# Three transformer mixers on one core: the slab of x, the raw weights and the temporary tiles move to the other end of the on-chip memory

## The chip, the cores and the metric

The kernel runs on one core of a Trainium2 chip. A core has five engines that run side by side: TensorE (PE, matmuls; its weight loads are listed as PEld), VectorE (DVE), ScalarE (ACT), GpSimd (POOL) and SyncE (SP, which issues most DMAs). They work on SBUF, an on-chip memory of 128 partitions; a tile takes the same bytes in each partition, and its address is the byte at which it begins there. The metric is the device time of one execution in microseconds (us), as the median of three runs; less is better.

## What is computed

Two programs in a row, on 512 tokens of 1024 features, in float32:

```
x = x + merged(windowed attention, gated convolution) @ w_out     # first mixer
x = x + moe(rmsnorm(x))           # 32 experts, 2 for each token
for layer in range(2):
    h = h + mixer(rmsnorm(h))     # two kinds of full attention; then neighbourhood attention
    h = h + relu(rmsnorm(h) @ w_up)**2 @ w_down     # w_up 1024 x 4096, w_down 4096 x 1024
out = rmsnorm(h)
```

## The kernel before

Features lie on partitions and the 512 tokens along the free dimension. Nearly all products are of 128 x 128 blocks of a weight with 128 x 512 blocks of activations. For precision each operand is kept as two float32r tiles, a rounded part and the rest: `wh` and `wl` for weights, `xh` and `xl` (or `uh` and `ul`, `mh` and `ml`, and so on) for activations. One block is then three matmuls into the same PSUM bank: `wh` with `xh`, `wh` with `xl`, `wl` with `xh` (`mm3`, lines 222 to 226). The 128 x 128 weight block is loaded into the array (PEld), and the 512 columns of the activation block are streamed through it.

Weights come as a stream that all phases draw from. `_dma` loads a job (1 MB for most) into one of three `raw` tiles; `_split` lets ScalarE round 512 columns of it into one of four `wh` tiles (line 122), and `_lows` lets VectorE put the rest into `wl` (line 131), a few blocks ahead of TensorE. `raw`, `wh` and `wl` are rings: a slot is used again as its last reader is done.

The phases are the first mixer (to about 340 us), the experts (to 650), the first full attention (to 910), the first feed-forward layer (to 1273), neighbourhood attention (to 1535) and the second feed-forward layer. In a feed-forward layer `ffn` alternates between `up`, in which 4 banks of 8 blocks each are formed from `xh` and `xl`, and `down`, in which 8 banks of 4 blocks each are formed from `uh` and `ul`; that is 96 matmuls in either. The experts use float32 weights straight from the buffers that the DMAs fill (`raw`, `ew`, `esH`, `esL`, `ey`, and the tiles `t`), 2 MB for each half of a pair's gate and up, and `comb` (line 1879) adds their results `y` through one-hot matrices `C`.

Space is given out by pools. A pool on the left side grows upwards from the pools opened before it, one on the right side downwards from the top. `const`, `slab`, `wp` and `tmp` stay open from start to end. The phase pools are opened and closed on top of them. So the sizes of the pools below set the address of everything above. In `slab` lie the two activation slabs H and L (`xh`, `xl`) and one more slab, tag X, which holds `x`, and at other times `xin`, `mg`, `pt` or `V`; in `wp` lie `raw`, `wh` and `wl`; in `tmp` lie twelve small tiles `few` of 160 bytes, `ss`, seven tiles `t`, three tiles `rcol` of 32 bytes, and `rstd`.

The order of the instructions is that in which the program is written (`manual_schedule`); nothing reorders them. The lines that the change touches are those that open pools (44 to 47) and those that allocate `raw` (53) and the X slab (858, 877, 1021, 1129, 1340, 1440).

Of the kernel before, what the change touches and what calls it, by code (L numbers as in the profile page):

```python
# [16 lines left out]
T = 512  # L17
# [9 lines left out]
class Row:  # L27
    """Tiles of 512 columns as one."""
# [9 lines left out]
class Core:  # L38
    """Pools, engines and the stream of weights that every phase draws from."""

    def __init__(self, ctx, tc, aps):
# [5 lines left out]
        self.tmp = ctx.enter_context(tc.tile_pool(name="tmp", bufs=1))  # L47
# [5 lines left out]
        raw = lambda: self.wp.tile([128, 2048], F32, name="raw", tag="raw", bufs=NRAW)  # L53
# [15 lines left out]
    def add_job(self, ap, blocks, split=True, ring=0):  # L69
        """One transfer; blocks: (width, count) of the blocks in it, in order. Returns what is to be added to groups."""  # L70
        j = len(self.jobs)
        self.jobs.append((ap, ring))
        gs, off = [], 0
        for w, n in blocks:
            if not split:
                gs.append((off, w * n, w))
                off += w * n
                continue
            while n:
                k = min(n, SPL // w)  # L80
                gs.append((off, w * k, w))
                off += w * k
                n -= k
        gs = [(j, o, n, w, split, i == len(gs) - 1) for i, (o, n, w) in enumerate(gs)]
        return gs
# [41 lines left out]
    def _lows(self, upto=None):  # L127
        """The second parts that are still to be formed, up to group upto."""
# [6 lines left out]
    def blk_w(self, ahead=NSPL - 1):  # L135
        """The next block of weights in two parts; what comes after it is split ahead."""
# [22 lines left out]
    def slab_ring(self):  # L159
        """A ring of the slabs of x in two parts, while they are free."""  # L160
# [23 lines left out]
    def run(self, main):  # L184
        """main, with self.ratio steps of the side work after each of its quanta; then what is left of the side work."""
# [12 lines left out]
    def later(self, n, f):  # L198
        """f, n quanta from now."""
        self.due.append([n, f])  # L200
# [27 lines left out]
    def block(self, nk, xh, xl, acc, first=True, last=True, x0=0, ahead=NSPL - 1):  # L228
        """acc += the next nk blocks of weights times the blocks of x from x0 on."""
# [6 lines left out]
    def split(self, src, h, l, scale=None, late=0, then=None):  # L236
        """src, scaled, in two parts, the second one late quanta after the first; then() after both."""
# [20 lines left out]
    def rsqrt(self, a, shape, out=None, pool=False):  # L258
        """a ** -0.5 of a few numbers: a guess on the exponent, a step of second order and one of third order."""
# [35 lines left out]
    def token_sums(self, s, w, n, t, o):  # L295
        """Sums over the features of s [128, T] with weights w [128, n], tokens on partitions, into t[:, o:]."""
# [3 lines left out]
    def more_sums(self, s, t, first, last):  # L300
        """The sums of one tile of several into t[:, :4]."""
# [4 lines left out]
    def norm_tokens(self, s, n=D):  # L306
        """rstd of every token, tokens on partitions: [128, 4]."""
# [13 lines left out]
    def rows(self, cols, t, p0=0, p1=128):  # L321
        """cols [128, 4 or less] as a row of tokens on the partitions p0..p1 of a bank."""
# [11 lines left out]
    def norm_begin(self, g0):  # L334
        """Slabs for g * x in two parts, and a function to call as each block of x is final."""
# [10 lines left out]
    def square(self, s, x, d, dve=False):  # L346
        """s (+)= x * x; s as a list takes the last block on its own."""
# [43 lines left out]
def ffn(c, X, H, L, s, finish, halves=False):  # L391
    """X += relu(h W_up)^2 W_down, h = the norm of x; finish(d) as block d is final."""
    nc = c.nc
    c.mark("ffn")
    with c.tc.tile_pool(name="ffn", bufs=1, reuse_waits="tile") as pool:
# [44 lines left out]
        def down_halves():  # L440
            """The last chunk for one half of the tokens, then for the other."""
# [34 lines left out]
def final(c, X, out):  # L476
    """Function to call as a block of half of the tokens is final; the norm of the half follows the last one."""
# [45 lines left out]
def blocks(w, mb, kb):  # L523
    """[kb, 128, mb, 128] view of a weight."""
    return w.reshape(kb, 128, mb, 128)
# [24 lines left out]
class Heads:  # L550
    """Blocks of two heads each: gain and rope now, the scale of their norms for all of them at once.

    The scale of a token's norm commutes with gain and rope; for q it is left to the softmax.
    """
# [5 lines left out]
    def take(self, acc, g, b, write):  # L560
        """Block b from PSUM."""
# [24 lines left out]
    def scales(self, rcol):  # L586
        """The norm's scale and the main norm's in one: [128, 4, 2 n], heads of all blocks."""
# [14 lines left out]
    def scale_k(self, r, f, kst, go):  # L602
        """r * the scale of its norms, f [128, 4, 2], into kst; then go()."""
# [16 lines left out]
def v_tokens(c, acc, V, rcol):  # L620
    """Two heads of v from features to tokens on partitions, scaled."""
# [13 lines left out]
def write_q(c, r, qst, pool=False):  # L635
    """Two heads, each with its two parts one above the other; qst [128, 2, T]."""
# [7 lines left out]
def write_k(c, r, kst):  # L644
    """Two heads, each part twice; kst [128, 2 heads, 2 parts, T]."""
# [14 lines left out]
def pairs_attn(c, units, scores, scale, pv, sink=None, lag=2, ready=None):  # L660
    """Softmax attention over head pairs.

    scores(u, hh, i, nm, p) returns the scores and puts -max * scale(u, hh, i) into nm.
    """
# [122 lines left out]
class WindowPV:  # L787
    """Products with v; room holds the transposed probabilities of three heads, in turn."""
# [63 lines left out]
def window(c):  # L852
    """The first mixer, and the router's part of the experts behind it."""
# [4 lines left out]
    xin = c.slab.tile([128, NB, T], F32, name="xin", tag="X")  # L858
# [18 lines left out]
    mg = c.slab.tile([128, NB, T], F32, name="mg", tag="X")  # L877
# [42 lines left out]
    def conv(j, x, y):  # L920
        """The three taps over x * y."""
# [96 lines left out]
    def start():  # L1018
        es1.close()
        c.moe = Moe(c)  # L1020
        return c.slab.tile([128, NB, T], F32, name="x", tag="X"), {d: xres[:, d] for d in range(NB)}
# [23 lines left out]
def load_res(c, xr, res):  # L1045
    """x before a mixer."""
# [5 lines left out]
def outproj(c, mh, ml, done, start, norm, nn, early=4):  # L1052
    """x = xr + W m, block by block, and the next norm behind it.

    The first two blocks run as the parts of m come, done() of them, and early - 2 more while the last part is awaited;
    start() gives x and xr when all are there.
    """
# [48 lines left out]
class Cat:  # L1106
    """Blocks of several tiles in a row."""
# [8 lines left out]
def l0(c, nn, accs, res, norm):  # L1116
# [12 lines left out]
    ptx = c.slab.tile([128, 2, 4, T], F32, name="pt", tag="X")  # L1129
# [32 lines left out]
    def latent(n, g0, tag, keep, after):  # L1162
        """Blocks with a norm of their own: keep(m, acc, gain) takes them, after() follows the scale of the norm."""
# [170 lines left out]
def after_attn(c, es, es1, res):  # L1334
    """x, and x before the mixer, in the room of the attention."""
# [4 lines left out]
    return c.slab.tile([128, NB, T], F32, name="x", tag="X"), xr  # L1340
# [46 lines left out]
class GridPV(WindowPV):  # L1387
    """Blocks of queries half a block behind those of keys: three of them see two blocks of keys each.

    The fourth has the last 64 tokens, which see the last block, and the first 64, which see the first one.  # L1390
    Transposed probabilities lie by blocks of keys, the first one last.
    """
# [28 lines left out]
def l1(c, nn, res, norm):  # L1421
# [18 lines left out]
    V = c.slab.tile([128, 4, D], F32, name="V", tag="X")  # L1440
# [115 lines left out]
def moe_jobs(c):  # L1556
    """Three pieces for each pair of experts: two halves of gate and up, and down; each in one transfer or two."""
# [25 lines left out]
def moe_order():  # L1583
    """The pieces as they are used: the gates and ups of a pair before the down of the one before."""
# [9 lines left out]
class Moe:  # L1594
# [28 lines left out]
    def norm(self):  # L1623
        """As Core.norm_begin, for the router: logits without the norm's scale and rows of x for the gathers."""
# [28 lines left out]
    def row(self, d, xd):  # L1653
        """Block d of x, tokens as rows, for the gathers."""
# [12 lines left out]
    def first(self, name, src, mx, desc, n):  # L1667
        """One-hot of the first of the largest."""
# [10 lines left out]
    def route(self, X):  # L1679
        """1 + the position of every token among those of every expert that takes it, else 0."""  # L1680
# [50 lines left out]
    def gates(self):  # L1731
        """Gates and the norm's scale of every token for every expert, and the largest count."""
# [41 lines left out]
    def onehot(self, n, pos):  # L1774
        """Slots of the tokens for n pairs of experts."""
# [5 lines left out]
    def slots(self, n, oh, idc, idg):  # L1781
        """1 + the token of the slots of n pairs of experts, 0 for none; for the gather the token, and 0 for none."""
# [15 lines left out]
    def slots2(self, n, oh, info, gate, rs):  # L1798
        """Gate and norm's scale of the same slots."""
# [27 lines left out]
    def gu(self, xt, w, rs):  # L1827
        """silu(x Wg) * (x Wu) of the slots of a pair of experts; w(): the next half of the weights of both."""
# [24 lines left out]
    def down(self, ht, ws, gate, Y):  # L1853
        """gate * (hid Wd) in two parts."""
# [17 lines left out]
    def comb(self, X, d, slots):  # L1872
        """Block d of x += the slots of some pairs: (Y, C) of each."""
# [9 lines left out]
    def beyond(self, X):  # L1883
        """The slots past the first CAP of every expert, for inputs that fill them."""
# [43 lines left out]
    def early(self):  # L1928
        """Weights of the first experts in the room for results."""
# [4 lines left out]
def moe(c, X, nn, next_g):  # L1934
# [45 lines left out]
    def w():  # L1980
        """The next piece of the weights of both experts of a pair."""
# [96 lines left out]
def feat3(w):  # L2078
    """[L, n] -> [128, L * n / 128]"""
# [3 lines left out]
def perm(x):  # L2083
    """tokens (row, col) -> (col, row)"""
# [3 lines left out]
def mblocks(w, order, per):  # L2088
    """Blocks of 128 columns in the given order, per of them a job: [jobs, 128, per * K]."""
# [6 lines left out]
def lay_out(w, early=4):  # L2096
    """Blocks in the order of outproj, 16 to a job."""
# [120 lines left out]
```

## Time and profile before

| | |
|---|---|
| time, median of 3 runs | 1901.78 us (1900.95 to 1902.89) |
| span of the profiled execution, first to last instruction | 1899.4 us |
| TensorE busy | 1839.3 us (97%) |
| VectorE, ScalarE, GpSimd busy | 1080.8, 724.5, 341.7 us |
| DMA | 257.08 MB, mean 135 GB/s over the span |

For the profiled execution the profile gives its span; the timed runs are other executions of the same program. Times in the rows are from the start of the span. Matmuls are pipelined: one begins before the one ahead of it ends, so the time that a run of them takes is read from starts, not from the length of one. [...]

### The profile page before, as it was taken

How to read it: one execution, taken by the hardware profiler on the slowest of the kernel's cores; microseconds unless marked ns; L12 is line 12 of the kernel's file. 1: busy time of each engine (PE TensorE's matmuls, PEld its weight loads, DVE VectorE, ACT ScalarE, POOL GpSimd, SP SyncE). 2: the span in 40 equal slices, each digit the busy share in tenths (PEclk: the TensorE clock that was granted, in tenths of full speed). 3: DMA queues.
4: the chain of work that ended last, by engine and by line, in shares of the span. 5: the costliest groups of instructions: out<-in, count | busy, mean ns of one | idle time of the engine just before them, and what ended most of it. 6: DMA issues, size and time to landing. Idle time of an engine off the chain costs nothing.

```text
span 1899.4 us, 23667 instructions
## 1 busy us (share of the span) xinstructions
PE 1839.3 (97%) x8890; PEld 1370.8 (72%) x8890; DVE 1080.8 (57%) x1956; ACT 724.5 (38%) x1418; POOL 341.7 (18%) x356
## 2 busy tenths in 40 slices
PE   7999999799999999999999999999999999999998
PEld 6777787534444686667888888878777788888887
DVE  7765446535333767774655555564766565555555
ACT  4444334211111456654433333333656443333334
POOL 5310003110000251001211111120444221111111
PEclk9999999799999999999999999999999999999999
DMA  5211436599999321211323223233222222222321
GB/s 189 75 51 67 139 134 240 186 353 424 423 422 386 99 75 41 60 41 70 111 89 111 89 89 102 98 121 112 79 57 59 94 103 95 105 89 90 110 89 45
DMA packets 67334, 257.08 MB, mean 135 GB/s; under 512 B 22224, under 2 KB 28752, under 8 KB 42128
## 3 DMA queue, kind: packets, MB, share of 16 engines
q1 hardware_dynamic: 54848, 227.41, 32.5%
q0 software_dynamic: 5712, 19.66, 3.2%
q10 hardware_dynamic: 6656, 8.45, 1.2%
q8 instruction: 72, 1.18, 0.3%
q14 instruction: 46, 0.38, 0.1%
HBM read 245.28 MB, written 8.39 MB: 134 GB/s over the span
## 4 chain that ended last, share of the span: by engine, by line
PE 58%; DVE 5%; ACT 2%; issue 1%; POOLq 0%; DVEq 0%; ACTq 0%
PE psacc L224 15%; PE psacc L225 15%; PE psacc L226 15%; PE psT L693 2%; PE psO L847 2%; DVE wl L131 1%; PE psT L324 1%; PE psO L1416 1%; PE psS L224 1%; PE psS L225 1%; PE psS L226 1%; PE psT L1408 1%; PE psS L1473 1%; PE psS L1157 1%; ACT p L680 1%
## 5 line engine op out<-in xcount | busy, mean ns | idle before, releaser
L131 DVE TENSOR_TENSOR wl<-raw,wh 128x512 fp32r<-128x512 f32 x466 | 404.2, 871 | 248.6 <-ACT wh L122 244.7
L224 PE MATMUL psacc<-xh,wh 128*128 128x512 f32 x1008 | 408.9, 406 | 6.1 <-ACT wh L122 5.5
L122 ACT CAST wh<-raw 128x512 fp32r<-128x512 f32 x466 | 286.1, 617 | 334.7 <-PE psacc L225 284.0
L225 PE MATMUL psacc<-xl,wh 128*128 128x512 f32 x1008 | 396.0, 393 | 1.0 <-DVE xl L248 0.9
L226 PE MATMUL psacc<-xh,wl 128*128 128x512 f32 x1008 | 396.0, 393 | 0.1
L224 PEld LDWEIGHTS psacc<-xh,wh 128*128 128x128 f32 x1008 | 190.7, 189 | 55.9 <-issue 14.2
L226 PEld LDWEIGHTS psacc<-xh,wl 128*128 128x128 f32 x1008 | 190.6, 189 | 42.0 <-DVE wl L131 0.7
L225 PEld LDWEIGHTS psacc<-xl,wh 128*128 128x128 f32 x1008 | 191.1, 190 | 35.3 <-DVE xl L248 2.3
L224 PE MATMUL psacc<-uh,wh 128*128 128x512 f32 x480 | 190.1, 396 | 2.2 <-DVE x L436 2.2
L225 PE MATMUL psacc<-ul,wh 128*128 128x512 f32 x480 | 189.8, 396 | 0.0
L226 PE MATMUL psacc<-uh,wl 128*128 128x512 f32 x480 | 189.8, 396 | 0.0
L404 POOL TENSOR_TENSOR t<-t,rstd 128x512 f32<-128x512 f32 x64 | 83.2, 1299 | 535.1 <-ACT t L403 535.1
L436 DVE TENSOR_TENSOR x<-psacc,x 128x512 f32<-128x512 f32 x120 | 82.7, 689 | 134.4 <-PE psacc L226 134.4
L362 POOL TENSOR_TENSOR ss<-ss,t 128x512 f32<-128x512 f32 (+1 forms) x56 | 69.7, 1244 | 262.6 <-ACT t L355 242.5
L224 PEld LDWEIGHTS psacc<-uh,wh 128*128 128x128 f32 x480 | 90.2, 188 | 25.1 <-issue 3.4
L226 PEld LDWEIGHTS psacc<-uh,wl 128*128 128x128 f32 x480 | 90.2, 188 | 21.9
L225 PEld LDWEIGHTS psacc<-ul,wh 128*128 128x128 f32 x480 | 90.2, 188 | 21.5
L240 ACT CAST uh<-t 128x512 fp32r<-128x512 f32 x64 | 39.8, 621 | 131.3 <-DVE t L405 131.3
L693 PE MATMUL psT<-cst,p 128*128 128x128 f32 x448 | 77.2, 277 | 12.9 <-ACT p L680 12.7
L693 PEld LDWEIGHTS psT<-cst,p 128*128 128x128 f32 x448 | 55.2, 140 | 42.2 <-ACT p L680 22.3
L403 ACT ACTIVATE t<-psacc 128x512 f32<-128x512 f32 x64 | 38.2, 597 | 80.8 <-PE psacc L226 80.8
L701 DVE COPY pt<-psT 128x256 f32<-128x256 f32 (+1 forms) x80 | 43.2, 540 | 39.2 <-PE psT L693 38.5
(461 smaller groups left out, 2791.2 us busy)
## 6 DMA issues: line engine op xcount, KB each, us to landing
raw<-ffn SPq DMA_DIRECT2D x64, 1024.0 KB, 4.8
ew<-e_w SPq DMA_DIRECT2D x15, 2048.0 KB, 12.7
raw<-e_w SPq DMA_DIRECT2D x20, 1024.0 KB, 12.0
esH<-e_w SPq DMA_DIRECT2D x8, 2048.0 KB, 14.4
esL<-e_w SPq DMA_DIRECT2D x8, 2048.0 KB, 14.0
raw<-w_in_a SPq DMA_DIRECT2D x8, 1024.0 KB, 6.6
raw<-od_qk SPq DMA_DIRECT2D x8, 1024.0 KB, 4.8
raw<-w_gccp SPq DMA_DIRECT2D x8, 768.0 KB, 4.2
```

Of the source, the lines that this page charges most:

```text
L122: nc.scalar.copy(h[:, :n], r)
L131: self.nc.vector.tensor_sub(l, r, h)
L224: nc.tensor.matmul(acc, wh, xh, start=first, stop=False)
L225: nc.tensor.matmul(acc, wh, xl, start=False, stop=False)
L226: nc.tensor.matmul(acc, wl, xh, start=False, stop=last)
L240: nc.scalar.copy(h, src)
L362: self.nc.gpsimd.tensor_add(s, s, q)
L403: nc.scalar.activation(r, acc, AF.Relu)
L404: nc.gpsimd.tensor_mul(r2, r, st["r2"])
L436: nc.vector.tensor_add(X[:, d], acc, X[:, d])
L693: nc.tensor.transpose(t[:, o:o + 128], p[:, m * 128:m * 128 + 128], c.ident)
L701: nc.vector.tensor_copy(dst, src)
```

## The change

Two pools are new, `xs` for the slab X and `wr` for `raw`, and they and `tmp` are opened on the right side. The rest of the diff renames the pool at each allocation and takes out comments and docstrings, which moves line numbers by two behind the new pools.

```
-        self.tmp = ctx.enter_context(tc.tile_pool(name="tmp", bufs=1))
+        self.xs = ctx.enter_context(tc.tile_pool(name="xs", bufs=1, side="right"))
+        self.wr = ctx.enter_context(tc.tile_pool(name="wr", bufs=1, side="right"))
+        self.tmp = ctx.enter_context(tc.tile_pool(name="tmp", bufs=1, side="right"))
...
-        raw = lambda: self.wp.tile([128, 2048], F32, name="raw", tag="raw", bufs=NRAW)
+        raw = lambda: self.wr.tile([128, 2048], F32, name="raw", tag="raw", bufs=NRAW)
...
-    xin = c.slab.tile([128, NB, T], F32, name="xin", tag="X")
+    xin = c.xs.tile([128, NB, T], F32, name="xin", tag="X")
...
-    mg = c.slab.tile([128, NB, T], F32, name="mg", tag="X")
+    mg = c.xs.tile([128, NB, T], F32, name="mg", tag="X")
...
-        return c.slab.tile([128, NB, T], F32, name="x", tag="X"), {d: xres[:, d] for d in range(NB)}
+        return c.xs.tile([128, NB, T], F32, name="x", tag="X"), {d: xres[:, d] for d in range(NB)}
...
-    ptx = c.slab.tile([128, 2, 4, T], F32, name="pt", tag="X")
+    ptx = c.xs.tile([128, 2, 4, T], F32, name="pt", tag="X")
...
-    return c.slab.tile([128, NB, T], F32, name="x", tag="X"), xr
+    return c.xs.tile([128, NB, T], F32, name="x", tag="X"), xr
...
-    V = c.slab.tile([128, 4, D], F32, name="V", tag="X")
+    V = c.xs.tile([128, 4, D], F32, name="V", tag="X")
```

Every engine has the same instructions in the same order as before, with the same waits; DMAs are the same too. What differs is the addresses, in bytes of a partition (tiles of one row have the same start; a range stands for a ring or for several tiles):

| tiles | before | after | remainder by 64, before and after |
|---|---|---|---|
| `xh` (H), `esH` | 18,432 | 18,432 | 0, 0 |
| `xl` (L), `esL` | 34,816 | 34,816 | 0, 0 |
| X: `x`, `xin`, `mg`, `pt`, `V` | 51,200 | 212,960 | 0, 32 |
| `raw`, 3 of 8,192 | 67,584 | 188,384 | 0, 32 |
| `wh`, 4 of 2,048; `C` | 92,160 | 51,200 | 0, 0 |
| `wl`, 4 of 2,048 | 100,352 to 108,544 | 59,392 to 67,584 | 0, 0 |
| `few`, `ss` | 108,544; 110,464 | 167,936; 169,856 | 0, 0 |
| `t`, 7 of 2,048 | 112,512 | 171,904 | 0, 0 |
| `rcol`, `rstd` | 126,848; 126,944 | 186,240; 186,336 | 0, 0; 32, 32 |
| first phase pool: `mh`, `qa`, `oh`, first `uh`, first `y`, `ey` | 128,992 | 67,584 | 32, 0 |
| `uh`, `ul` in all, to their end | 128,992 to 178,144 | 67,584 to 116,736 | 32, 0 |
| `ml`, `ob` | 145,376 | 83,968 | 32, 0 |
| `ew`, first of two | 183,392 | 121,984 | 32, 0 |
| `qst` | 188,384 | 126,976 | 32, 0 |
| `chl` | 204,768 | 143,360 | 32, 0 |

The phase pools as a whole move down by 61,408 bytes, which is 64 x 959.5. Before, they begin behind `rstd`, at 63 x 2,048 - 32 = 128,992; after, they begin behind `wl`, at 33 x 2,048 = 67,584.

## Rows read from the trace of the kernel before

**Rows 1.** the page, part 1: busy us (share of the span), instructions of each engine
```profile
PE 1839.3 (97%) x8890; PEld 1370.8 (72%) x8890; DVE 1080.8 (57%) x1956; ACT 724.5 (38%) x1418; POOL 341.7 (18%) x356
```

**Rows 2.** stages in windows: busy us and count of each engine, granted clock, DMA
```profile
345.00:370.00 25.00, 15.20 (x91) 11.41 (x89) 14.71 (x64) 5.83 (x11) 3.87 (x4) 0.71 0.47 153
...
550.00:600.00 50.00, 50.00 (x235) 22.91 (x232) 18.95 (x31) 7.13 (x13) 1.89 (x2) 1.00 1.02 423
...
910.00:1240.00 330.00, 330.00 (x1445) 269.83 (x1444) 180.92 (x252) 109.29 (x189) 44.17 (x34) 1.00 0.28 96
...
1540.00:1899.00 359.00, 350.20 (x1628) 290.35 (x1627) 193.51 (x292) 122.15 (x219) 50.66 (x44) 0.99 0.25 88
```

**Rows 3.** the chain that ended last, from 960 to 1048 us, shares by line
```profile
by line: PE psacc L224 33.5%; PE psacc L225 33.5%; PE psacc L226 33.4%
```

**Rows 4.** timeline of TensorE: start us, us, line, tiles written and read
```profile
982.71 0.39 PE L224 MATMUL psacc<-xh,wh 128*128 128x512 f32 x1
...
1004.27 0.39 PE L226 MATMUL psacc<-xh,wl 128*128 128x512 f32 x1
1004.50 0.40 PE L224 MATMUL psacc<-uh,wh 128*128 128x512 f32 x1
...
1026.90 0.39 PE L224 MATMUL psacc<-xh,wh 128*128 128x512 f32 x1
```

**Rows 5.** groups of TensorE's matmuls in 982.8 to 1004.4 us (count, busy us, mean ns)
```profile
L224 PE MATMUL psacc<-xh,wh 128*128 128x512 f32 x32 | 12.5, 389 | 0.0
```

**Rows 6.** the same groups in 1004.6 to 1026.8 us
```profile
L224 PE MATMUL psacc<-uh,wh 128*128 128x512 f32 x32 | 12.7, 396 | 0.0
```

**Rows 7.** one tile's instructions in a window: those that read or write qst
```profile
276.52:298.92 22.40, 22.40 (x96) 17.84 (x95) 0.00 (x0) 0.00 (x0) 1.00 0.72 282
```

**Rows 8.** groups over the whole span, matmuls of 512 columns
```profile
L224 PE MATMUL psacc<-xh,wh 128*128 128x512 f32 x1008 | 408.9, 406 | 6.1 <-ACT wh L122 5.5 <-ACT t L566 0.6
...
L224 PE MATMUL psacc<-uh,wh 128*128 128x512 f32 x480 | 190.1, 396 | 2.2 <-DVE x L436 2.2
...
L1879 PE MATMUL psS<-C,y 128*128 128x512 f32 x224 | 59.4, 407 | 0.0
...
L224 PE MATMUL psacc<-mh,wh 128*128 128x512 f32 x64 | 25.8, 402 | 0.8 <-DVE t L1029 0.7
...
L224 PE MATMUL psacc<-oh,wh 128*128 128x512 f32 x48 | 20.0, 416 | 1.3 <-ACT oh L240 1.3
...
L224 PE MATMUL psacc<-chl,wh 128*128 128x512 f32 x32 | 13.4, 418 | 0.0
...
L224 PE MATMUL psacc<-qa,wh 128*128 128x512 f32 x24 | 10.2, 424 | 0.0
...
L224 PE MATMUL psacc<-ob,wh 128*128 128x512 f32 x24 | 9.7, 403 | 0.0
```

**Rows 9.** timeline of TensorE in the first mixer, other shapes between the triples
```profile
100.76 0.38 PE L693 MATMUL psT<-cst,p 128*128 128x128 f32 x2
100.90 0.48 PE L224 MATMUL psacc<-xh,wh 128*128 128x512 f32 x1
101.21 0.39 PE L225 MATMUL psacc<-xl,wh 128*128 128x512 f32 x1
101.44 0.40 PE L226 MATMUL psacc<-xh,wl 128*128 128x512 f32 x1
101.68 0.39 PE L224 MATMUL psacc<-xh,wh 128*128 128x512 f32 x1
```

**Rows 10.** DMA issues in 370 to 630 us: KB each, median us to landing
```profile
ew<-e_w SPq DMA_DIRECT2D x13, 2048.0 KB, 12.6
...
esH<-e_w SPq DMA_DIRECT2D x7, 2048.0 KB, 14.4
```

**Rows 11.** groups over the whole span, VectorE and ScalarE on weights
```profile
L131 DVE TENSOR_TENSOR wl<-raw,wh 128x512 fp32r<-128x512 f32 x466 | 404.2, 871 | 248.6 <-ACT wh L122 244.7 <-DVEq L1889 2.8
...
L122 ACT CAST wh<-raw 128x512 fp32r<-128x512 f32 x466 | 286.1, 617 | 334.7 <-PE psacc L225 284.0 <-PE psS L225 17.3 <-PE psO L1493 14.1
```

## The prediction

> **What bounds the kernel now.** I read the page's part 1 first, then the stages, then the chain in one stage, then the timeline of the engine that it names. TensorE is busy for 97% of the span and the next engine, VectorE, for 57% [rows 1]. In the stages with most of the time TensorE has no gap: 330.00 of 330.00 us in the first feed-forward layer, where VectorE works 180.92, ScalarE 109.29 and the DMA engines 28% of the time [rows 2]. The chain that ended last runs there over nothing but the three matmuls of `mm3` (lines 224 to 226) [rows 3]. So in these stages the time is a count of matmuls times the interval from the start of one to the start of the next. The change keeps the count; whatever it does to the time it does through this interval, or through another engine that becomes late.
>
> The interval differs between two loops of the same code. From 982.71 to 1004.50 us the layer's `up` runs 96 matmuls that stream `xh` and `xl` through weights `wh` and `wl`; from there to 1026.90 us `down` runs 96 that stream `uh` and `ul` through the same weight tiles [rows 4], 32 on each of the three lines [rows 5, 6]. That is 21.79 us / 96 = 226.9 ns against 22.40 us / 96 = 233.4 ns, a difference of 6.4 ns or 2.8%, with the same shapes, types, clock and order, and each matmul lasts 389 against 396 ns [rows 5, 6]. The 96 matmuls on `qst` in the first mixer take 22.40 us too, so 233.4 ns [rows 7], and this is another phase with other work on the other engines. What `uh`, `ul` and `qst` share, and `xh`, `xl` do not, is where they lie. By the table of addresses ahead, these tiles, like the others of the phase pools in it, start 32 bytes off a multiple of 64, because the first phase pool starts at 128,992 (63 x 2,048 - 32), and they lie at 128,992 or above; the slabs and the weight tiles start at multiples of 2,048 and end below 108,545.
>
> **The change part by part.** No instruction, DMA or wait is added, removed or reordered, so the whole sum is about durations at new addresses.
>
> (a) Phase pools down. They now start at 67,584 = 33 x 2,048, so `uh`, `ul`, `mh`, `ml`, `qa`, `oh`, `ob`, `chl` and `qst` stand to `wh` and `wl` as `xh` does. I take it that they then run at `xh`'s interval. `down`: 3 x 480 = 1,440 matmuls of 512 columns [rows 8] x 6.45 ns = 9.3 us. The others that stand in long triples: `qst` 96 [rows 7], and three lines each of `mh` 64, `oh` 48, `chl` 32, `qa` 24, `ob` 24, which makes 192 + 144 + 96 + 72 + 72 [rows 8]; together 672 x 6.45 = 4.3 us. All stand on TensorE's own chain, so nothing hides them. Bounds for this term: nothing, if the interval has another cause, and 15.0 us with all of (b).
>
> (b) Short runs. The steady interval needs a run. In the first mixer, where two small transposes come between triples, even `xh` goes 0.31, 0.23, 0.24 us from start to start [rows 9], on tiles that are aligned already. The 224 matmuls on `C`, with the misaligned `y` as weights [rows 8], come in runs of eight among other shapes, in a stage where TensorE is busy 50.00 of 50 us and the DMA engines are full as well, at 423 GB/s [rows 2]. Their bounds are 0 and 224 x 6.45 = 1.4 us; by the nearest row, that of `xh` between other shapes, I take 0.
>
> (c) `xh`, `xl`, `wh`, `wl`. The slabs stay; the weight tiles go from 92,160 to 51,200, both multiples of 2,048. A block of `xh` is 2,048 bytes and eight of them in turn meet four weight tiles at the same 389 ns [rows 5], so no multiple of 2,048 within 16 KiB matters to the interval. I take 0. Bounds: the 3 x 1,008 matmuls [rows 8] at 6.45 ns, so 19.5 us lost, or as much as a new steady state might gain, which no row shows.
>
> (d) `raw`, `x`, the temporary tiles. `raw` and `x` now start 32 bytes off a multiple of 64, which the big weight buffers `ew` (183,392) already did and `esH` (18,432) did not. Their 2 MB loads land in 12.6 and 14.4 us, the misaligned one no later [rows 10], so the loads cost 0. ScalarE reads `raw` for 617 ns and VectorE for 871 ns a tile [rows 11]; in the feed-forward layer VectorE could take 149 us more and ScalarE 221 us more before they fill the stage [rows 2]. Cost 0; for this cover to be gone, these instructions would have to take well over half as long again.
>
> Sum: 9.3 + 4.3 = 13.6 us. The profiled execution's span is 1899.4 us and the median of the timed runs 1901.78, so 2.4 us lie around the span; they stay. 1899.4 - 13.6 + 2.4 = 1888.2, predicted 1888 us.
>
> [...]
>
> **The rivals.**
> - Height, not offset. All slow tiles also lie at 128,992 or above, and all fast ones below 108,545. Then `uh`, `ul`, `mh`, `ml`, `oh`, `qa`, `ob` gain, since they come to lie at 67,584 to 116,736, but `qst` (126,976) and `chl` (143,360) do not: 9.3 + 480 x 6.45 = 12.4 us, 1889 us. For it: every row fits it as well as the offset does. Against it: the first block of `uh`, just above the weight tiles, is no faster than the rest, as one mean of 396 ns over all four shows [rows 6]. It has the same sign and nearly the same size.
> - No change, 1902 us. The interval would come from what `down` does besides, such as VectorE's additions out of PSUM, and not from addresses. Against it: `qst` has the same 233.4 ns without that work [rows 7]. [...]
> - Slower, by nearness. The streamed tile and the weights would disturb each other the more the closer they lie. The last block of `xl` is 43,008 bytes from the first weight tile now and 2,048 afterwards; the first block of `uh` is 20,448 bytes beyond the last weight tile. Then `uh` stays slow and `xh`, `xl` become slow too, in the projections and in `up`: 3,024 x 6.45 = 19.5 us more, 1921 us. It decides as soon as `xh`'s interval grows by 4.5 ns, which eats the 13.6 us. Against it: `ul` reaches 178,144, far from the weights, and is as slow as `uh`.
>
> **How the numbers follow.** Offset 0.66 (1888), height 0.18 (1889), no change 0.10 (1902), nearness 0.06 (1921). A measurement of this kernel can tell 0.2%, 3.8 us, from no change; the first two cases are faster by more, so faster 0.84, same 0.10, slower 0.06. Below 1888 the range takes in the 1.4 us of (b), and 3 us more for the same shapes where they stand in shorter runs and settle sooner once neighbours no longer differ: 1883. There is one more loose piece: from 345 to 370 us the granted clock averages 0.71 [rows 2], after TensorE's busy share fell to 15.20 of 25 us; that costs 25 x 0.29 = 7.3 us, and where the stage begins a little earlier I allow a third of it, some 2 us either way. Above, it takes in that only half of `down`'s gain is real and nothing of the rest, 4.7 us: 1897. So 1883 to 1897.
>
> **What would show it.** In the changed profile: 96 matmuls of `down` in 21.8 us in place of 22.4, each at 389 ns; the run on `qst` in 21.8 us (offset) or still 22.4 us (height); `up` unchanged at 21.8 us; VectorE's and ScalarE's means within a few per cent, and TensorE without a new gap in the feed-forward layers. I am wrong if `down` still takes 233 ns, if `up` takes more than 227 ns, or if TensorE begins to wait for `wh`, `wl` or for `raw`.

## The result and the profile after

The changed kernel takes 1889.82 us (median of 4 runs, 1886.21 to 1891.23) against 1902.34 us for the kernel before in the same comparison; the ratio is 0.9929 with a 95% interval of 0.9915 to 0.9943. The forecast was 1888 us, in a range of 1883 to 1897.

Part 1 of the page of the changed kernel answers to [rows 1]:

```profile
PE 1824.1 (97%) x8890; PEld 1369.5 (73%) x8890; DVE 1080.7 (57%) x1956; ACT 724.4 (38%) x1418; POOL 342.3 (18%) x356
```

The number of instructions is the same. TensorE is busy for 15.2 us less and the span went from 1899.4 to 1887.1 us, 12.3 us less; the other engines work as long as before. The timeline of TensorE in the first feed-forward layer shows where (start us, us, line, tiles); line 226 is now what line 224 was [rows 4]:

```profile
959.72 0.39 PE L226 MATMUL psacc<-uh,wh 128*128 128x512 f32 x1
...
981.48 0.39 PE L226 MATMUL psacc<-xh,wh 128*128 128x512 f32 x1
...
1003.24 0.39 PE L226 MATMUL psacc<-uh,wh 128*128 128x512 f32 x1
```

The 96 matmuls of `down` run from 959.72 to 981.48 us, 21.76 us in place of 22.40, and the 96 of `up` behind them take 21.76 us too, in place of 21.79. Both are 226.7 ns from start to start. The groups of the next `down`, from 1003.3 to 1024.9 us, have the length that only `xh` had [rows 5, 6]:

```profile
L226 PE MATMUL psacc<-uh,wh 128*128 128x512 f32 x32 | 12.4, 389 | 0.0
```

The window of the 96 matmuls on `qst`, in the first mixer, answers to [rows 7]; its end is now 21.76 us behind its start:

```profile
276.29:298.05 21.76, 21.76 (x96) 17.83 (x95) 0.00 (x0) 0.00 (x0) 1.00 0.74 290
```

What was to cost nothing cost nothing. These are the groups of VectorE and ScalarE on the weights, as in [rows 11], and the DMA issues of the experts, as in [rows 10]:

```profile
L133 DVE TENSOR_TENSOR wl<-raw,wh 128x512 fp32r<-128x512 f32 x466 | 403.3, 869 | 245.8 <-ACT wh L124 241.8 <-DVEq L1891 2.8
...
L124 ACT CAST wh<-raw 128x512 fp32r<-128x512 f32 x466 | 285.8, 617 | 323.4 <-PE psacc L227 273.6 <-PE psS L227 16.5 <-PE psO L1495 14.1
```

```profile
ew<-e_w SPq DMA_DIRECT2D x13, 2048.0 KB, 11.2
...
esH<-e_w SPq DMA_DIRECT2D x7, 2048.0 KB, 13.1
```

`raw` is read from 188,384 as fast as from 67,584 (869 and 617 ns, before 871 and 617), and `ew`, which went from a remainder of 32 to one of 0, lands 1.4 us sooner while `esH`, which did not move, lands 1.3 us sooner; the order between the two is as before.

By stages, from the starts of the same instructions in the two traces:

| up to | before, us | after, us | lead, us |
|---|---|---|---|
| first matmul on `qst` | 276.52 | 276.29 | 0.23 |
| last run on `mh` in the first mixer | 348.84 | 347.49 | 1.35 |
| last pair of experts, first half of gate and up | 591.84 | 590.69 | 1.15 |
| first projection of the full attention | 660.95 | 660.94 | 0.01 |
| first `down` | 960.31 | 959.72 | 0.59 |
| first long run of neighbourhood attention | 1318.57 | 1313.22 | 5.35 |
| second feed-forward layer | 1540.64 | 1533.37 | 7.27 |
| end of its last full `down` | 1863.64 | 1851.72 | 11.92 |
| end of the span | 1899.4 | 1887.1 | 12.3 |

The feed-forward layers give 4.8 and 4.7 us, neighbourhood attention 1.9, the first mixer 1.4, the full attention 0.6. All of the first mixer's lead is gone again by the first projection behind the experts. The stage windows bear on where it goes: first the kernel before (its window from 345 to 370 us is in [rows 2]), then the changed one (us; busy us and count of PE, PEld, DVE, ACT, POOL; granted clock; DMA share; GB/s).

```profile
370.00:400.00 30.00, 26.07 (x132) 10.76 (x133) 11.64 (x31) 3.98 (x6) 2.71 (x2) 0.85 0.88 342
400.00:450.00 50.00, 47.87 (x280) 21.76 (x279) 23.61 (x59) 7.03 (x13) 4.65 (x4) 1.00 0.99 399
...
600.00:650.00 50.00, 46.02 (x196) 26.53 (x195) 30.19 (x43) 16.25 (x28) 6.39 (x5) 0.97 0.45 166
```

```profile
345.00:370.00 25.00, 13.85 (x88) 10.67 (x87) 15.01 (x66) 5.82 (x11) 3.87 (x4) 0.77 0.53 171
370.00:400.00 30.00, 26.55 (x153) 10.97 (x153) 12.59 (x36) 4.35 (x7) 3.22 (x3) 0.90 0.91 362
400.00:450.00 50.00, 48.03 (x262) 21.35 (x260) 22.54 (x51) 6.66 (x12) 4.15 (x4) 0.97 0.98 393
...
600.00:650.00 50.00, 45.73 (x192) 26.57 (x188) 29.47 (x42) 16.28 (x28) 6.40 (x5) 0.93 0.43 154
```

The granted clock, a share of full speed, is higher than before from 345 to 370 us (0.77 against 0.71) and from 370 to 400 (0.90 against 0.85), and lower from 400 to 450 (0.97 against 1.00) and from 600 to 650 (0.93 against 0.97). The lead follows: by the starts of the same instructions it is 2.5 us at 400 us, 0.8 at 420, 1.2 at 630 and 0.2 at 640. So 1.3 us are lost in this stage, together with the clock; that the clock is the cause is argued and not shown, as no run holds it fixed. The same stretch loses 1.4 to 1.5 us in the traces of two kernels with padding alone and of one with the weights shifted by 256 bytes (experiments below), and 1.4 us in that with the weights shifted by 64, whose matmuls are slow; so the loss does not hang on the fast interval. It lies within the 2 us that the forecast had allowed for the clock, though not in the window that it named, 345 to 370 us, where the clock rose.

### The profile page after: what moved, and what is told of

It reads as the page before. It is cut to its first block, busy times and chain, and to the rows that moved or that the text cites. A ratio compares the mean times of both kernels' runs of the same rounds, so it can differ in the third digit from the quotient of the medians.

```text
span 1887.1 us, 23667 instructions
## 1 busy us (share of the span) xinstructions
PE 1824.1 (97%) x8890; PEld 1369.5 (73%) x8890; DVE 1080.7 (57%) x1956; ACT 724.4 (38%) x1418; POOL 342.3 (18%) x356
## 4 chain that ended last, share of the span: by engine, by line
PE 56%; DVE 6%; ACT 2%; issue 1%; DMA 0%; POOL 0%; POOLq 0%; DVEq 0%; ACTq 0%
PE psacc L226 15%; PE psacc L228 15%; PE psacc L227 14%; PE psT L695 2%; PE psO L849 2%; DVE wl L133 1%; PE psT L326 1%; PE psO L1418 1%; PE psT L1410 1%; PE psS L1475 1%; PE psS L226 1%; PE psS L1159 1%; PE psS L227 1%; PE psS L228 1%; ACT p L682 1%
```

## Experiments

**The offset without the way down.** An unused tile of 32 bytes behind `tmp` in the kernel before. The left phase pools then start at 129,024 and stay high; `qst` and `chl` hang from the top and stay where they were, so they serve as the control.

```
+        self.pad = ctx.enter_context(tc.tile_pool(name="pad", bufs=1))
+        self.pad.tile([128, 8], F32, name="pad", tag="pad")
```

> The kernel before with one unused tile of 32 bytes behind the temporary tiles: nothing moves down, but the left phase pools (uh, ul, mh, ml, qa, oh, ob, y) start at 129,024, a multiple of 64; qst and chl, which hang from the top, stay 32 off. Offset theory: the 96 matmuls of down take 21.8 us instead of 22.4, the run on qst stays at 22.4; 9.6 us from down and 480 x 6.7 ns = 3.2 us from the others, so 1889.5 us. Height theory (it is the way down that counts): down stays at 22.4 us, 1902 us.

Measured: 1891.02 us, ratio to the kernel before 0.9931 (0.9914 to 0.9947), as good as the whole change. The timeline at the start of `down`, of `up` and of the next `down`, and behind it the window of the run on `qst`:

```profile
960.07 0.39 PE L226 MATMUL psacc<-uh,wh 128*128 128x512 f32 x1
...
981.83 0.39 PE L226 MATMUL psacc<-xh,wh 128*128 128x512 f32 x1
...
1003.59 0.39 PE L226 MATMUL psacc<-uh,wh 128*128 128x512 f32 x1
```

```profile
276.35:298.75 22.40, 22.40 (x96) 17.85 (x95) 0.00 (x0) 0.00 (x0) 1.00 0.74 282
```

`down` takes 21.76 us at 129,024, and `qst`, which did not move, 22.40. Height is out: 32 bytes further up, `uh` is fast.

**The way down without the offset.** The same unused 32 bytes behind `wl` in the changed kernel, so that the left phase pools start at 67,616.

> The changed kernel with one unused tile of 32 bytes behind wl: the left phase pools start at 67,616, low but 32 off a multiple of 64; qst (126,976) and chl stay where they were. Offset theory: down takes 22.4 us again, qst stays at 21.8, up at 21.8; 1889.8 + 9.6 + 3.2 = 1902.6 us. Height theory: down stays at 21.8 us, 1890 us.

Measured: 1901.31 us, ratio to the kernel before 0.9989 (0.9980 to 0.9999). The same places:

```profile
961.66 0.40 PE L228 MATMUL psacc<-uh,wh 128*128 128x512 f32 x1
...
984.06 0.40 PE L228 MATMUL psacc<-xh,wh 128*128 128x512 f32 x1
```

```profile
277.39:299.15 21.76, 21.76 (x96) 17.83 (x95) 0.00 (x0) 0.00 (x0) 1.00 0.75 290
```

`down` is back at 22.40 us; `qst` and `chl`, which the pad does not reach, keep their gain (the median interval on `chl`, which stands in shorter runs, is 231 ns as in the changed kernel, and 234 in the kernel before). The two pads together show the effect with the sign either way, with `raw`, `x` and `tmp` at the bottom and at the top.

**Whose offset.** Two kernels, each the changed one with 32 unused bytes at another place: ahead of the slabs, which shifts slabs, weights and left phase pools alike, and ahead of the weights with 32 more behind them, which shifts the weights alone.

> The changed kernel with the unused 32 bytes ahead of the slabs: xh, xl, wh, wl and the left phase pools are all 32 off, qst and chl are not. If the offset that counts is that of either tile to a multiple of 64: up and down at 22.4 us, qst as well (its weights are off), some 1889.8 + 9.6 + 3.2 + 18 = 1921 us. If it is the offset between the streamed tile and the weights: up and down at 21.8 us, qst and chl at 22.4 us, some 1891 us.

> The changed kernel with 32 unused bytes ahead of wh and wl and 32 behind them: the weight tiles alone are 32 off, everything that is streamed through them is at a multiple of 64. If the offset between the two tiles counts, or that of either: up, down and qst all at 22.4 us, some 1921 us. If only the offset of the streamed tile counts: all at 21.8 us, 1890 us.

Measured, one run each: 1892.92 and 1914.88 us. First the kernel with everything shifted, `down` and `up`, then its run on `qst`:

```profile
961.63 0.39 PE L228 MATMUL psacc<-uh,wh 128*128 128x512 f32 x1
...
983.39 0.39 PE L228 MATMUL psacc<-xh,wh 128*128 128x512 f32 x1
...
1005.15 0.39 PE L228 MATMUL psacc<-uh,wh 128*128 128x512 f32 x1
```

```profile
277.92:300.32 22.40, 22.40 (x96) 17.85 (x95) 0.00 (x0) 0.00 (x0) 1.00 0.73 282
```

And the kernel with the weights alone shifted:

```profile
963.95 0.40 PE L230 MATMUL psacc<-uh,wh 128*128 128x512 f32 x1
...
986.35 0.39 PE L230 MATMUL psacc<-xh,wh 128*128 128x512 f32 x1
...
1008.74 0.40 PE L230 MATMUL psacc<-uh,wh 128*128 128x512 f32 x1
```

Where both tiles are 32 off, both loops take 21.76 us, and the run on `qst`, whose own tile is now the aligned one, takes 22.40. Where only the weights are off, `down` takes 22.40 and `up` 22.39 us, `up` for the first time. So no tile has a right place by itself; what counts is the distance between the weights and the tile that is streamed through them.

The 1914.88 us lie 6 us below the expected 1921. The expectation counted all matmuls on `xh` alike; against the trace of the kernel before, the stages that hold the two feed-forward layers lose 9.4 us, and the first mixer, the full attention and neighbourhood attention, where many of these matmuls stand between other shapes, together 5.5.

A rival is that ScalarE and VectorE, which write the next `wh` and `wl` meanwhile, disturb the streamed reads. The trace of the kernel before speaks against it: in the `down` from 1004.50 us, 38 intervals that lie in such writes for over four fifths average 233.2 ns, and 33 that meet none average 233.5. The addresses of the weights and of the streamed tile act together on the interval, by 6.7 ns on top of 226.7; through what they act was not shown.

**How long the period is.** The offset of 32 left open whether 64 is the period. Four kernels give each weight slot 64 bytes of room, so that slots lie 2,112 bytes apart, and put the weights 0, 16, 48 and 8 bytes into the slot. The code shown is that for 0 bytes.

```
-                h = self.wp.tile([128, SPL], F32R, name="wh", tag="wh", bufs=NSPL)
-                l = self.wp.tile([128, SPL], F32R, name="wl", tag="wl", bufs=NSPL)
+                h = self.wp.tile([128, SPL + 16], F32R, name="wh", tag="wh", bufs=NSPL)[:, 0:0 + SPL]
+                l = self.wp.tile([128, SPL + 16], F32R, name="wl", tag="wl", bufs=NSPL)[:, 0:0 + SPL]
```

> The changed kernel with 64 bytes of room behind each wh and wl slot: all tiles of TensorE stay at multiples of 64, but the slots now differ by 64 in their remainder by 128 and 256. If only the offset by 64 counts: up, down and qst at 21.8 us, 1890 us. If a longer period counts (128 or more): intervals that change from slot to slot, some of them above 226.7 ns, and a time above 1892 us.

> As the kernel with 64 bytes of room behind each weight slot, and the weights put 16 bytes into the slot, so 16 off a multiple of 64 against everything streamed. If the offset acts in halves of 32 bytes: as with 0 off, 21.8 us for 96 matmuls, 1890 us. If it acts in finer steps: an interval between or beside 226.7 and 233.4 ns, that is 21.4 to 22.4 us, 1870 to 1915 us.

> The same with the weights 48 bytes into the slot. Halves of 32 bytes: as with 32 off, 22.4 us for 96 matmuls, 1915 us. Finer steps: another value; if the distance to the next multiple of 64 is what counts, the same as 16 off.

> The same with the weights 8 bytes into the slot. Halves of 32 bytes: as with 0 off, 21.8 us, 1890 us. [...]

Measured, one run each: 1907.40, 1913.69, 1910.30 and 1912.89 us. With 0 bytes, where every tile is still at a multiple of 64, both loops take 22.20 us:

```profile
962.58 0.39 PE L226 MATMUL psacc<-uh,wh 128*128 128x512 f32 x1
...
984.78 0.39 PE L226 MATMUL psacc<-xh,wh 128*128 128x512 f32 x1
...
1006.98 0.39 PE L226 MATMUL psacc<-uh,wh 128*128 128x512 f32 x1
```

So multiples of 64 do not suffice. A slot serves 12 matmuls, and the four slots lie 0, 64, 128 and 192 bytes off a multiple of 256. The timeline at the starts of three slots, with the fifth matmul of the first of them (second line):

```profile
965.36 0.40 PE L226 MATMUL psacc<-uh,wh 128*128 128x512 f32 x1
...
966.29 0.39 PE L227 MATMUL psacc<-ul,wh 128*128 128x512 f32 x1
...
968.10 0.39 PE L226 MATMUL psacc<-uh,wh 128*128 128x512 f32 x1
...
970.89 0.39 PE L226 MATMUL psacc<-uh,wh 128*128 128x512 f32 x1
```

The slot from 965.36 us takes 2.74 us, its last eight matmuls 1.81 us; the slot behind it takes 2.79 us, and the one ahead of it, from 962.58 us, 2.78. Over 24 rounds of the ring from 962.58 us the last eight matmuls of a slot average 226.5 ns in this one slot, and 232.5 to 233.1 ns in the other three. So three of four slots are slow; that the fast one is the slot at a multiple of 256 fits, but the trace does not name slots.

The other three kernels lie at 232.4, 231.5 and 232.9 ns in both loops. The same averages are 230.5 to 234.5 ns there, and no slot reaches 226.7, although in each kernel one of the four is exactly 16, 48 or 8 bytes off a multiple of 256. So these offsets are not free either; what each of them costs by itself is not separated. ScalarE and VectorE write the tiles that start 8 bytes into a slot as fast as those of the changed kernel, 618 and 868 ns against 617 and 869.

In three more kernels the whole weight ring is shifted by one constant, with the rest of 512 bytes behind it. The code shown is that for 64 bytes; for 128 and 256 the tiles have 32 and 96, and 64 and 64 numbers.

```
+        self.pad = ctx.enter_context(tc.tile_pool(name="pad", bufs=1))
+        self.pad.tile([128, 16], F32, name="pad", tag="pad")
         self.wp = ctx.enter_context(tc.tile_pool(name="wp", bufs=1))
+        self.pad2 = ctx.enter_context(tc.tile_pool(name="pad2", bufs=1))
+        self.pad2.tile([128, 112], F32, name="pad2", tag="pad2")
```

> The changed kernel with 64 unused bytes ahead of the weight ring and 448 behind it: every wh and wl slot is 64 off a multiple of 512 against everything streamed, the same for all slots. If the constant offset counts by 64 alone, and the kernel with slots 2112 bytes apart lost its 226.7 ns because its offset changes from slot to slot: 21.8 us for 96 matmuls, 1890 us. If the period is 128 or more: another steady interval, above 226.7 ns by what that kernel shows (231 to 233 ns), 1905 to 1913 us.

> The same with 128 bytes ahead and 384 behind. Period 64 or 128: 21.8 us for 96 matmuls, 1890 us. Period 256 or more: another steady interval, 1895 to 1913 us.

> The same with 256 bytes ahead and 256 behind. Period 64, 128 or 256: 21.8 us for 96 matmuls, 1890 us. Period 512 or more: another steady interval.

Measured, one run each: 1917.58, 1915.38 and 1890.24 us. The first two starts of `down` and `up`, for 64, 128 and 256 bytes:

```profile
967.56 0.40 PE L230 MATMUL psacc<-uh,wh 128*128 128x512 f32 x1
...
989.96 0.40 PE L230 MATMUL psacc<-xh,wh 128*128 128x512 f32 x1
```

```profile
967.67 0.39 PE L230 MATMUL psacc<-uh,wh 128*128 128x512 f32 x1
...
989.98 0.39 PE L230 MATMUL psacc<-xh,wh 128*128 128x512 f32 x1
```

```profile
961.00 0.39 PE L230 MATMUL psacc<-uh,wh 128*128 128x512 f32 x1
...
982.76 0.39 PE L230 MATMUL psacc<-xh,wh 128*128 128x512 f32 x1
```

The run of 96 takes 22.40, 22.31 and 21.76 us. Offsets of 32, 64 and 128 bytes cost 6.7, 6.7 and 5.7 ns a matmul, 256 costs nothing. A constant offset of 64 makes the kernel 27 us slower than 256 does, and 13.5 us slower than the kernel before on the same chip (1904.03). The times for 64 and 128 lie above those expected (up to 1913 us).

**All of it by padding.** The kernel before with 32 unused bytes behind `tmp` and 224 at the top, which brings every tile that is streamed through `wh` and `wl` to a multiple of 256 from them.

```
+        self.pad = ctx.enter_context(tc.tile_pool(name="pad", bufs=1))
+        self.pad.tile([128, 8], F32, name="pad", tag="pad")
+        self.pad2 = ctx.enter_context(tc.tile_pool(name="pad2", bufs=1, side="right"))
+        self.pad2.tile([128, 56], F32, name="pad2", tag="pad2")
```

> The kernel before with two unused tiles and no move: 32 bytes behind the temporary tiles (left phase pools at 129,024) and 224 bytes at the top (pools that hang from there 224 lower, so qst at 188,160 and chl at 204,544). Every tile that is streamed through wh and wl then stands at a multiple of 256 from them; raw, x and the temporary tiles stay low. If the offset is the whole effect: down, up and qst at 21.8 us, ratio to the kernel before 0.993, as the change has. If moving raw, x and the temporary tiles away adds something of its own: down and qst at 21.8 us, but a ratio nearer to 1 than the change has.

Measured: 1890.22 us, ratio 0.9926 (0.9908 to 0.9943). `down` and the run on `qst`:

```profile
960.05 0.39 PE L228 MATMUL psacc<-uh,wh 128*128 128x512 f32 x1
...
981.81 0.39 PE L228 MATMUL psacc<-xh,wh 128*128 128x512 f32 x1
```

```profile
276.53:298.29 21.76, 21.76 (x96) 17.83 (x95) 0.00 (x0) 0.00 (x0) 1.00 0.74 290
```

256 bytes that nobody reads do what the move of three pools does. The move adds nothing of its own that can be measured: 0.9926 and 0.9929 have intervals that nearly coincide. No version tried beats the changed kernel by more than these intervals.

## Why the prediction was right

- **That the interval of TensorE is the bound and depends on addresses** was right. The two loops of the same code pointed to it before any run, and 22.40 us for 96 matmuls became 21.76; that it is the address was shown by the pads.
- **(a) `down`, 9.3 us.** From the first `down` to neighbourhood attention the lead grows from 0.59 to 5.35 us, in the second layer from 7.27 to 11.92: 9.4 us. The interval fell by 6.7 ns and not by 6.45, as `up` too lost the slow matmuls at its start: 21.79 us became 21.76.
- **(a) the other triples, 4.3 us.** The first mixer, the full attention and neighbourhood attention gave 1.35 + 0.58 + 1.92 = 3.9 us. The run on `qst` gave its full 0.64.
- **(b) short runs, 0 taken out of 0 to 1.4.** From 431 to 592 us, where the experts run in a steady cycle, the lead grew by 0.3 us.
- **(c) and (d), 0.** The interval of `xh` stayed, and so did the instructions on `raw` and the order of the loads.
- **What made 12.3 us of 13.6.** The stages outside the experts give 13.3 us up to the end of the last full `down` and 0.4 behind it; the experts' stage, where the clock differs, takes 1.3 away.
- **The wrong part of the reasoning** is the unit. The prediction has the tiles "stand to `wh` and `wl` as `xh` does", but what it reads off and forecasts by is each tile's own remainder by 64. The runs show that the distance to the weights counts; an offset of 64 costs as much as one of 32, and 128 nearly as much. That the forecast came out all the same was luck: the new addresses happen to be multiples of 256 throughout, 18,432, 34,816, 51,200, 67,584, 83,968, 126,976 and 143,360. Had the pools come to lie at 67,648, the same reasoning would have given 1888 us, and by the run with an offset of 64 (argued, as this kernel was not run) `down` would have stayed slow.
- **The rivals.** Height fell with the two pads, and so did the case of no change. Nearness fell with the changed kernel itself, in which the weights begin where `xl` ends and `up` takes 21.76 us.

## What to carry to other kernels

Where TensorE is the bound, read the interval from start to start of long runs of one shape, and compare runs that differ only in their tiles; a difference of 3% there was worth 12 us here. For float32r matmuls of 128 x 512 with a weight load each, place the weight tiles and everything that is streamed through them at distances that are multiples of 256 bytes (226.7 ns here, against 232.4 to 233.3 at 32, 64 and 128 bytes off them), and look at the addresses again after any change to a small pool: here 32 bytes that were missing ahead of the phase pools cost some 12 us. A gain that follows a move of buffers should be checked with an unused tile of a few bytes before it is put down to the region of the memory.

## What the runs showed of the hardware

- The interval of back-to-back float32r matmuls of 128 x 512 with a weight load each, at a granted clock of 1.00, is 226.7 ns where the weights lie a multiple of 256 bytes from the streamed tile, 233.3 ns with the weights 32 bytes above such a place (kernel before) or 32 below it (left phase pools at 67,616), 233.3 at 64 above and 232.4 at 128. The fast interval is the same for streamed tiles from 18,432 (`xh`) to 188,160 (`qst` in the last kernel), and the tile's own remainder by 64 does not matter (both tiles at 0, or both at 32).
- In the changed kernel the long run that begins behind another shape at 1533.4 us starts with an interval of 315 ns and six of 228 to 236 ns, then has 226 and 227. Where the slots of the weights differ in their offset, as at 2,112 bytes apart, one slot of four settles at 226.5 ns and the mean is 231.3.
- Whether it is the loading of the next weights beside the running matmul that does this, why multiples of 256 are free, and what the offsets 8, 16, 48, 96, 160 and 192 give each by itself, was not settled. None of the constant offsets tried gave an interval below 226.7 ns.
